# Norm-side weight splits, modulation buffers and transposes of a two-block fp32 network in another order

## The chip, the cores and the metric

The kernel runs on one core of a Trainium2 chip. The metric is the device time of one execution in microseconds; the kernel before was run three times. TensorE multiplies, VectorE, ScalarE and GpSimd do the elementwise work, and SyncE (SP) issues nearly all DMAs from one queue that is served in order. Each engine works through its own row of instructions in a fixed order and waits on semaphores for the others.

## The reference

The input is 512 tokens of width 1024, a context of 256 tokens, and weights, all in fp32. The first block has two layers; the context goes through the first of them and is only read by the second.

```python
for l in range(2):
    mod = silu(c) @ w_mod[l] + b_mod[l]                      # six rows: shift, scale, gate, twice
    px = (rmsnorm(x, norm1_g) * (1 + sc1) + sh1) @ w_in      # mLSTM, gating unit, convolution from px
    x = x + g1 * (y_x @ w_out)
    x = x + g2 * swiglu(rmsnorm(x, norm2_g) * (1 + sc2) + sh2, w_gu, w_down)
x = rmsnorm(x, final_g)
for i in range(2):                                           # mixer A: 3 dilated windows; mixer B: sinks
    h = mixer_a(x, ...) if i == 0 else mixer_b(x, ...)
    x = layer_norm(ALPHA * x + h, ln_g[i], ln_b[i])
    gate = sigmoid(x @ ple_w_gate[i])
    x = x + gate * (p[i] @ ple_w_proj[i])
```

## The kernel before

**Products.** Every fp32 factor is split into a high part (rounded to the format that TensorE takes at full rate) and the rest, the low part; a product is the sum of three matmuls (high by high, high by low, low by high). For a weight block, `wblock` loads it in two halves of 128 x 1024 (`raw`, three buffers), ScalarE copies `hi` (L121) and VectorE subtracts `lo` (L124). Activations are split into `Hh` and `Hl` after they have been transposed on TensorE (`finish_T`, L354; `split_T`, L417; `to_T`, L397). Matmuls and transposes are recorded on the lines of these helpers, L138 for all matmuls.

**Tokens.** They are worked on in chunks of 128: six in layer 0 (four of the input, two of the context), four from then on. `pend` holds functions that transpose and split a chunk once its norm is there; `pend.upto(c)` issues those up to chunk c, so its place in the code says where the transposes stand among TensorE's matmuls.

**Order.** The code is written as one program, and a scheduler places the instructions of each engine by priority, by code order first; `behind(es)` holds the instructions of a block back until the last split recorded for ScalarE ("A") or VectorE ("V") or the last GpSimd instruction ("G") has been issued. Loads are asked for on SP in the order in which the code reaches them, and each waits until its buffer is free.

**The places of the change, in the order of the program.** (1) The FFN of each layer starts with a product that is interleaved with the transposes of its last chunks: `fm_pair` in layer 0, `fm_pairs` in layer 1; `fm_pair` also computes mixer B's keys. (2) `mod_gen` computes one of the six modulation rows: four loads of 1 MB into one buffer `wm`, and 16 small matmuls (32 columns of weights wide) on each; these groups (`md<-wm`) are strewn through the FFN by `modl.pump`. (3) `resid` multiplies a product by the gate row on VectorE (`ot`) and adds it to the residual stream `w` on GpSimd, in quarters of 256 columns. (4) `chunkf` is the norm behind layer 1: scale and gain in two halves, VectorE one, ScalarE and GpSimd the other; the chunk is then transposed for mixer A. (5) Mixer A has four quads of heads by three windows, twelve rounds; `a_pieces` gives the products of a round, `a_stages` the attention of it, and `weave` lays the products of a round between the attention of the round before. `first` is the product of the first round, interleaved with the transposes of the last chunks. (6) After each mixer, `post_attention` adds the output product and normalises, and `embed_gate` computes the gate product in two column halves n, each from two weight halves kh. `affine` multiplies a chunk by the layer norm's gain `lg` (GpSimd) and adds its bias `lb` (VectorE); `use` multiplies the gate `pg` with the projected embedding `pq` and adds it to `w`. The block for (n, kh) = (0, 1), `early`, has buffers of its own and is asked for before `embed_gate`. The stage behind mixer A is called gate 0 here, that behind mixer B gate 1.

## Time and profile before

| | us |
|---|---|
| median of 3 runs (lowest, highest) | 2639.34 (2638.47, 2640.25) |
| the profiled execution | 2640.76 |
| its span (and what lies around it) | 2638.7 (2.06) |
| TensorE busy | 2561.2, 97% of the span |
| VectorE, ScalarE, GpSimd busy | 1329.4, 973.2, 572.6 |

The profile is of one execution. The granted clock is a share of TensorE's full speed (2.4 GHz): 1.00, or 0.50 where it is at its lower level of 1.2 GHz; over the whole span it is 0.99. A row of a timeline gives the start, the duration, the engine, the line, the operation with output and inputs, how many follow one another, and in brackets how long the engine was idle before and what ended that. DVE is VectorE, ACT ScalarE, POOL GpSimd.

### The profile page before, as it was taken

Reading aid. Unit: us, or ns where it says so; the run is one execution under the profiler, and the core shown is the slowest. Engines: PE = TensorE matmul, PEld = TensorE weight load, DVE = VectorE, ACT = ScalarE, POOL = GpSimd, SP = SyncE. Lnnn points to the kernel's source line nnn. Section 1 sums busy time; section 2 is a strip of 40 time slices with the busy share of each in tenths; the row PEclk is TensorE's granted clock in tenths of the full one; section 3 lists DMA queues with packets and bytes.
Section 4 is the critical chain, followed back from the end, with each engine's and each line's share of the span. In section 5 each row is a group of like instructions: output and inputs, shape, how many; then the busy total and the mean of one; then the engine's idle time right before and its main releaser. Section 6 shows DMA issues by size and latency. Waiting matters only on the chain.

```text
span 2638.7 us, 39880 instructions
## 1 busy us (share of the span) xinstructions
PE 2561.2 (97%) x15408; PEld 2163.5 (82%) x15408; DVE 1329.4 (50%) x2858; ACT 973.2 (37%) x2034; POOL 572.6 (22%) x614
## 2 busy tenths in 40 slices
PE   7999999999999999999999999999999999989998
PEld 5888788788888888887978888888888888768777
DVE  4675664142323335766543443534454545665666
ACT  3424444021121225345522222434343445434753
POOL 1175532020302013034220120411111111021102
PEclk9999999999999999999999999999999999999999
DMA  8421553443212123227342332433434443524352
GB/s 304 132 72 41 158 197 120 167 148 123 74 56 72 60 67 112 79 77 215 120 156 84 104 100 80 140 105 99 140 111 136 119 135 112 176 92 138 118 168 64
DMA packets 132286, 314.74 MB, mean 119 GB/s; under 512 B 18785, under 2 KB 49089, under 8 KB 132097
## 3 DMA queue, kind: packets, MB, share of 16 engines
q1 hardware_dynamic: 132096, 312.20, 37.7%
q8 instruction: 121, 1.98, 0.3%
q14 instruction: 69, 0.56, 0.1%
HBM read 272.02 MB, written 13.89 MB: 108 GB/s over the span
## 4 chain that ended last, share of the span: by engine, by line
PE 86%; DVE 4%; DMA 4%; ACT 3%; POOL 2%; issue 1%; SPq 0%; DVEq 0%; POOLq 0%; ACTq 0%
PE mm L138 72%; PE md L138 5%; PE tr L138 5%; PE tr L1272 1%; DMA wm<-in_w_mod_dram 1%; DMA t<-mwd 1%; ACT t L121 1%; DVE lo L124 1%; PE tr L354 1%; POOL w L124 1%; DVE w L124 0%; DVE t L124 0%; POOL t L124 0%; ACT hi L121 0%; DMA w<-in_x_dram 0%
## 5 line engine op out<-in xcount | busy, mean ns | idle before, releaser
L138 PE MATMUL mm<-Hh,hi 128*128 128x512 f32 (+1 forms) x2208 | 798.8, 362 | 7.8 <-ACT hi L121 3.9
L138 PE MATMUL mm<-Hl,hi 128*128 128x512 f32 (+1 forms) x2208 | 772.6, 360 | 0.2 <-DVE Hl L124 0.2
L138 PE MATMUL mm<-Hh,lo 128*128 128x512 f32 (+1 forms) x2208 | 712.9, 360 | 1.4 <-DVE lo L124 1.4
L121 ACT ACTIVATE hi<-raw 128x1024 fp32r<-128x1024 f32 (+1 forms) x350 | 341.6, 1003 | 777.4 <-PE mm L138 364.7
L124 DVE TENSOR_TENSOR lo<-raw,hi 128x1024 fp32r<-128x1024 f32 (+1 forms) x350 | 427.9, 1237 | 272.6 <-ACT hi L121 272.5
L138 PEld LDWEIGHTS mm<-Hh,hi 128*128 128x128 f32 x2208 | 416.6, 189 | 99.0 <-ACT hi L121 4.7
L138 PEld LDWEIGHTS mm<-Hl,hi 128*128 128x128 f32 x2208 | 417.3, 189 | 65.3 <-issue 1.6
L138 PEld LDWEIGHTS mm<-Hh,lo 128*128 128x128 f32 x2208 | 381.5, 189 | 49.8 <-issue 4.2
L124 POOL TENSOR_TENSOR w<-w,ot 128x256 f32<-128x256 f32 x200 | 170.7, 877 | 839.9 <-DVE ot L124 838.5
L124 DVE TENSOR_TENSOR sg<-mm,sg 128x512 f32<-128x512 f32 (+1 forms) x132 | 75.9, 600 | 407.4 <-PE mm L138 231.5
L138 PE MATMUL mm<-hi,Hh 128*128 128x256 f32 (+2 forms) x740 | 224.1, 303 | 4.8 <-ACT Hh L121 4.6
L138 PE MATMUL mm<-hi,Hl 128*128 128x256 f32 (+2 forms) x740 | 220.2, 298 | 1.0 <-POOL Hl L124 1.0
L138 PE MATMUL mm<-lo,Hh 128*128 128x256 f32 (+2 forms) x740 | 219.2, 296 | 2.0 <-DVE lo L124 2.0
L124 POOL TENSOR_TENSOR qr<-rt,rt 128x512 f32<-128x512 f32 x58 | 81.7, 1424 | 487.0 <-DVE rt L124 341.6
L138 PEld LDWEIGHTS mm<-hi,Hh 128*128 128x128 f32 x740 | 140.6, 190 | 12.6 <-ACT Hh L121 5.1
L138 PEld LDWEIGHTS mm<-hi,Hl 128*128 128x128 f32 x740 | 140.5, 190 | 6.5 <-issue 1.2
L138 PEld LDWEIGHTS mm<-lo,Hh 128*128 128x128 f32 x740 | 140.4, 190 | 6.3 <-DVE lo L124 2.4
L138 PE MATMUL mm<-hi,ah 128*128 128x512 f32 x352 | 139.7, 397 | 0.0
L138 PE MATMUL mm<-lo,ah 128*128 128x512 f32 x352 | 139.4, 396 | 0.0
L138 PE MATMUL mm<-hi,al 128*128 128x512 f32 x352 | 139.3, 396 | 0.0
L138 PE MATMUL mm<-hi,Yh 128*128 128x256 f32 (+1 forms) x416 | 129.3, 312 | 4.0 <-DVE t L124 2.6
L138 PE MATMUL mm<-hi,Yl 128*128 128x256 f32 (+1 forms) x416 | 128.2, 308 | 0.0
(369 smaller groups left out, 3666.7 us busy)
## 6 DMA issues: line engine op xcount, KB each, us to landing
raw<-in_w_gu_dram SPq DMA_DIRECT2D x88, 512.0 KB
raw<-in_a_in_dram SPq DMA_DIRECT2D x72, 512.0 KB
wm<-in_w_mod_dram SPq DMA_DIRECT2D x24, 1024.0 KB
raw<-in_w_in_dram SPq DMA_DIRECT2D x40, 512.0 KB
raw<-in_w_mod_dram SPq DMA_DIRECT2D x36, 512.0 KB
raw<-in_w_d_dram SPq DMA_DIRECT2D x24, 512.0 KB
raw<-in_w_d_dram SPq DMA_DIRECT2D x40, 256.0 KB
t<-mwd SPq DMA_DIRECT2D x38, 256.0 KB
```

What stands on the lines that cost most here:

```text
L121: return S.activation(o, i, f, **kw)
L124: return (e or V).tensor_tensor(out=o, in0=x, in1=y, op=op)
L138: lasts["P"] = PE.matmul(o, lhsT=l, rhs=r, start=start, stop=stop, **kw).ins
L354: PE.transpose(pt[:, 128 * m:128 * m + 128], src(4 * i + m), ident)
L1272: PE.transpose(pt[:, 128 * i:128 * i + 128], e, ident)
```

## The change

- `fm_pair` issues the transposes of the next two chunks ahead of the second product (m = 1) on the present two, where they stood behind it; `fm_pairs` issues the last chunk's ahead of the second weight block.
- `mod_gen` gets two `wm` buffers.
- `resid` adds the last chunk's quarters 2 and 3 on VectorE, in the residual addition and in the last FFN group; `chunkf` multiplies the last chunk's second half by the gain on VectorE.
- In `first`, the first weight block of mixer A is no longer held behind the last split; the second one is.
- `weave` calls `ahead` before the last piece of a round: it asks for the first weight block of the next round.
- `affine` does both steps on VectorE, held behind its last split; the block (0, 1) of `embed_gate` is made where it is used, behind the last norm's split on ScalarE and VectorE.

```diff
             for q in range(0, n, 256):
-                pend.upto((o + q) // 128 + 1)
                 for m in range(2):
+                    pend.upto((o + q) // 128 + (3 if m else 1))
                     fm_into([pss[m][i][:, q:q + 256]], wb, 128 * m, H, [(o + q, 256)])
...
             for i, wb in enumerate(wbs):
-                pend.upto(first + i if q == 0 else 9)
+                pend.upto(first if i + q == 0 else 9)
                 for m in range(2):
...
             for kh, c in order:
-                if kh not in wb:
-                    wb[kh] = {(0, 0): first, (0, 1): early}.get((n, kh)) or wblock(src[n, kh], nk, 512)
+                if kh not in wb and (n, kh) == (0, 1) and early:
+                    pend.upto(9)
+                    with behind():
+                        wb[kh] = early()
+                elif kh not in wb:
+                    wb[kh] = (n + kh == 0 and first) or wblock(src[n, kh], nk, 512)
                 hi, lo = wb[kh]
...
         for kp in range(8 // kn):
-            wm = (T(pool, [128, 2, 1024], "wm", bufs=1) if pool
+            wm = (T(pool, [128, 2, 1024], "wm", bufs=2) if pool
                   else T(wp, [128, 1024], "raw", bufs=3).rearrange("p (k n) -> p k n", k=1))
...

-        def resid(pool, c, n, ps, g):
+        def resid(pool, c, n, ps, g, final=True):
             tmp = T(pool, [128, 256], "ot", bufs=3)
...
             tt(tmp, ps, g[:, sl], MUL)
-            tt(xt[c][:, sl], xt[c][:, sl], tmp, ADD, e=G)
+            tt(xt[c][:, sl], xt[c][:, sl], tmp, ADD, e=V if final and n >= 2 and c == chs[-1] else G)

...
                 for n in (2 * n2, 2 * n2 + 1):
-                    resid(FP, c, n, ps[:, 256 * (n % 2):256 * (n % 2) + 256], g2[c // 4])
+                    resid(FP, c, n, ps[:, 256 * (n % 2):256 * (n % 2) + 256], g2[c // 4], lastg)
                     if lastg:
...
         act(xt[:, 512:1024], xt[:, 512:1024], AF.Copy, scale=rs)
-        tt(xt[:, 512:1024], xt[:, 512:1024], fg[0][:, 512:1024], MUL, e=G)
+        tt(xt[:, 512:1024], xt[:, 512:1024], fg[0][:, 512:1024], MUL, e=V if c == 3 else G)
         ld(xf[c], xt)
...
         def affine(c):
-            with behind("G"):
-                tt(xt[c], xt[c], lg, MUL, e=G)
-            tt(xt[c], xt[c], lb, ADD)
+            with behind("V"):
+                tt(xt[c], xt[c], lg, MUL)
+                tt(xt[c], xt[c], lb, ADD)

...

-    def weave(pieces, stages):
+    def weave(pieces, stages, ahead=noop):

...
         for i, p in enumerate(pieces):
+            if i == np_ - 1:
+                ahead()
             p()
...
                 if m == 0:
-                    wb[i] = wblock(a["a_in"][g, Q, i], 8, 256)
+                    if i not in wb:
+                        wb[i] = wblock(a["a_in"][g, Q, i], 8, 256)
                     d["p", i, 0] = fm(wb[i], 0, HA, SEGS_X)[0]
...

+            wb[0] = wblock(a["a_in"][g, Q, 0], 8, 256)
             with behind("AV"):
-                wb[0] = wblock(a["a_in"][g, Q, 0], 8, 256)
-            wb[1] = wblock(a["a_in"][g, Q, 1], 8, 256)
+                wb[1] = wblock(a["a_in"][g, Q, 1], 8, 256)
             ps = [mmt() for _ in range(3)]
...
             return [first, qk(1, 1)] + vs
+
+        def ahead():
+            i = 1 if g == 0 else 0
+            wb[i] = wblock(a["a_in"][g, Q, i], 8, 256)
+
+        d["ahead"] = ahead
         return [qk(i, m) for i in ((1, 0) if g == 0 else (0, 1)) for m in range(2)] + vs
...
     quad = None
-    for (Q, g) in its:
+    zt = {}
+
+    def z_ahead():
+        zt["w"] = wblock(a["a_z"][0], 8, 256)
+
+    ds = [{} for _ in its]
+    rounds = [a_pieces(Q, g, d) for (Q, g), d in zip(its, ds)]
+    for k, (Q, g) in enumerate(its):
         if g == 0:
             nquad = {"st": T(S2, [128, 3, 2, 4, 4], "qst", bufs=2)}
-        d = {}
-        pieces = a_pieces(Q, g, d)
+        d, pieces = ds[k], rounds[k]
         if prev is None:
-            for p in pieces:
-                p()
+            weave(pieces, [], ds[k + 1]["ahead"])
         else:
-            weave(pieces, prev + late)
+            weave(pieces, prev + late, ds[k + 1]["ahead"] if k < 11 else z_ahead)
             late = []
...
         prev_qg, prev_quad = (Q, g), nquad
-    zt = {}

...
         def f():
-            if pr % 2 == 0:
+            if pr % 2 == 0 and pr:
                 zt["w"] = wblock(a["a_z"][pr // 2], 8, 256)
...
     early = T(HBp, [128, 2, 4, 512], "Hh", F32R, bufs=1)
-    early = wblock(a["ple_g"][0, 0, 1], 4, 512, (early[:, 0], early[:, 1]))
+    eh = early[:, 0], early[:, 1]
     HB = []
...

-    embed_gate(0, H, PO, xt, affine, done_a, early)
+    embed_gate(0, H, PO, xt, affine, done_a, lambda: wblock(a["ple_g"][0, 0, 1], 4, 512, eh))
     close(PO)
...
     WX = opened("wx", "right")
-    early = wblock(a["ple_g"][1, 0, 1], 4, 512, [T(WX, [128, 4, 512], t, F32R) for t in ("hi", "lo")])
-    embed_gate(1, H, PO, xt, affine, done_b, early)
+    ew = [T(WX, [128, 4, 512], t, F32R) for t in ("hi", "lo")]
+    embed_gate(1, H, PO, xt, affine, done_b, lambda: wblock(a["ple_g"][1, 0, 1], 4, 512, ew))
     close(PO)
```

What this does to the order of the instructions is shown at three places, in the names of the built programs. First SP's queue in layer 0's FFN, at the modulation loads that precede the rows at 520 to 526 us; `wm` are modulation loads, `raw` with `w_d` and `w_gu` FFN weights. Before:

```order
L281 DMA wm_5267<-in_w_mod_dram 128x2x1024
L159 DMA raw_5482<-in_w_d_dram 128x512
L159 DMA raw_5560<-in_w_gu_dram 128x1024
L281 DMA wm_5670<-in_w_mod_dram 128x2x1024
L281 DMA wm_5680<-in_w_mod_dram 128x2x1024
L281 DMA wm_5820<-in_w_mod_dram 128x2x1024
L159 DMA raw_5564<-in_w_gu_dram 128x1024
L159 DMA raw_5707<-in_w_gu_dram 128x1024
L159 DMA raw_5711<-in_w_gu_dram 128x1024
```

After:

```order
L285 DMA wm_5267<-in_w_mod_dram 128x2x1024
...
L285 DMA wm_5670<-in_w_mod_dram 128x2x1024
L159 DMA raw_5482<-in_w_d_dram 128x512
L159 DMA raw_5560<-in_w_gu_dram 128x1024
L285 DMA wm_5680<-in_w_mod_dram 128x2x1024
L285 DMA wm_5820<-in_w_mod_dram 128x2x1024
L285 DMA wm_5830<-in_w_mod_dram 128x2x1024
L159 DMA raw_5564<-in_w_gu_dram 128x1024
L159 DMA raw_5707<-in_w_gu_dram 128x1024
L159 DMA raw_5711<-in_w_gu_dram 128x1024
```

The second load of the group (wm_5680) is still the one behind wm_5670, but each load is now queued one load further ahead of its use, and wm_5830 stands ahead of the FFN weights raw_5564 to raw_5711.

Next ScalarE at the FFN start of layer 1; `xs_12083` is the second half of the last chunk's scaled rows, `hi_12384` the high part of a weight block, `Hh` that of activations. Before:

```order
L121 ACTIVATE t_1767_12057<-tr_12052,modc_15_99,modc_16_100 128x128 x4
L121 ACTIVATE jk_12050,ss_11671<-w_11533 128x256
L121 ACTIVATE Hh_11519<-t_1767_12057 128x4x128
L121 ACTIVATE Hh_11519<-t_1769_12069 128x4x128
L121 ACTIVATE hi_12384<-raw_12386 128x1024
L121 ACTIVATE xs_12083<-w_11533,rs_12078 128x512
L121 ACTIVATE hi_12384<-raw_12390 128x1024
L121 ACTIVATE t_1787_12208<-tr_12203,modc_15_99,modc_16_100 128x128 x4
L121 ACTIVATE Hh_11519<-t_1787_12208 128x4x128
```

After:

```order
L121 ACTIVATE hi_12086<-raw_12092 128x1024
L121 ACTIVATE t_1767_12057<-tr_12052,modc_15_99,modc_16_100 128x128 x4
L121 ACTIVATE Hh_11519<-t_1767_12057 128x4x128
L121 ACTIVATE jk_12050,ss_11671<-w_11533 128x256
L121 ACTIVATE hi_12384<-raw_12386 128x1024
L121 ACTIVATE Hh_11519<-t_1769_12069 128x4x128
L121 ACTIVATE hi_12384<-raw_12390 128x1024
L121 ACTIVATE xs_12083<-w_11533,rs_12078 128x512
L121 ACTIVATE t_1787_12160<-tr_12155,modc_15_99,modc_16_100 128x128 x4
```

`xs_12083`, which the transposes of the last chunk read, has moved behind both halves of `hi_12384`.

Last VectorE in gate 0; `w_20625` to `w_20631` are chunks 0 to 3, `lo_21227` and `lo_21237` the low parts for the second column half. Before:

```order
L124 TENSOR_TENSOR Hl_20617<-t_3158_20992,Hh_20616 128x4x128
L1317 BN_AGGR mv_21011<-lst_20769 128x2
L124 TENSOR_TENSOR lo_21227<-raw_21232,hi_21226 128x1024
L131 TENSOR_SCALAR rv_21014<-mv_21011 128x1
L124 TENSOR_TENSOR lo_21237<-raw_21238,hi_21236 128x1024
L127 SCALAR_TENSOR_TENSOR nb_21017<-mv_21011,rs_21013 128x1
L133 TENSOR_SCALAR w_20631<-w_20631,mv_21011,rs_21013 128x512
L124 TENSOR_TENSOR lo_21237<-raw_21242,hi_21236 128x1024
L133 TENSOR_SCALAR t_3178_21089<-tr_21084,lncol 128x128 x4
L124 TENSOR_TENSOR Hl_20617<-t_3176_21077,Hh_20616 128x4x128
L124 TENSOR_TENSOR w_20625<-w_20625,lb_20622 128x1024
L124 TENSOR_TENSOR w_20627<-w_20627,lb_20622 128x1024
```

After, at the norm and, behind the dots, after the gating of the first column half:

```order
L1321 BN_AGGR mv_21011<-lst_20769 128x2
L131 TENSOR_SCALAR rv_21014<-mv_21011 128x1
L127 SCALAR_TENSOR_TENSOR nb_21017<-mv_21011,rs_21013 128x1
L133 TENSOR_SCALAR w_20631<-w_20631,mv_21011,rs_21013 128x512
L124 TENSOR_TENSOR lo_21227<-raw_21232,hi_21226 128x1024
L133 TENSOR_SCALAR t_3176_21081<-tr_21076,lncol 128x128 x4
L124 TENSOR_TENSOR Hl_20617<-t_3174_21069,Hh_20616 128x4x128
L124 TENSOR_TENSOR w_20625<-w_20625,lg_20621 128x1024
...
L124 TENSOR_TENSOR w_20631<-w_20631,pg_21214 128x256
L124 TENSOR_TENSOR w_20631<-w_20631,pg_21220 128x256
L124 TENSOR_TENSOR lo_21237<-raw_21238,hi_21236 128x1024
L124 TENSOR_TENSOR lo_21237<-raw_21242,hi_21236 128x1024
```

Between the statistics (`mv`) and the scaled chunk 3 no weight's low part is left; `lo_21237` has moved behind the affine steps and the gating of all four chunks.

## Rows read from the trace of the kernel before

**Rows 1.** The page: engine busy line and chain that ended last.

```profile
PE 2561.2 (97%) x15408; PEld 2163.5 (82%) x15408; DVE 1329.4 (50%) x2858; ACT 973.2 (37%) x2034; POOL 572.6 (22%) x614
...
PE 86%; DVE 4%; DMA 4%; ACT 3%; POOL 2%; issue 1%; SPq 0%; DVEq 0%; POOLq 0%; ACTq 0%
```

**Rows 2.** Who waited for whom, TensorE: us in total, times, longest.

```profile
PE md L138 <- DMA wm<-in_w_mod_dram: 6.1, 3, 5.3
...
PE tr L397 <- DVE w L124: 5.3, 1, 5.3
```

**Rows 3.** Stretches: length, busy us of PE, PEld, DVE, ACT, POOL, granted clock, DMA share.

```profile
429.40:432.80 3.40, 3.18 (x15) 3.11 (x15) 2.62 (x3) 2.87 (x4) 1.28 (x1) 0.50 0.64 251
526.50:535.20 8.70, 8.11 (x31) 5.42 (x32) 2.74 (x6) 1.75 (x3) 0.09 (x1) 0.50 0.48 136
1678.70:1685.40 6.70, 4.95 (x22) 4.56 (x23) 6.00 (x7) 4.93 (x7) 2.77 (x2) 0.50 0.29 98
2358.50:2361.30 2.80, 2.80 (x9) 2.33 (x10) 1.47 (x3) 0.60 (x1) 0.00 (x0) 0.50 0.76 281
2593.40:2596.90 3.50, 3.46 (x12) 3.10 (x13) 2.53 (x6) 2.57 (x7) 0.00 (x0) 0.51 0.00 0
```

**Rows 4.** Timeline of TensorE at layer 0's FFN start: start, us, idle before in brackets.

```profile
425.76 0.28 PE L138 MATMUL mm<-Hh,hi 128*128 128x256 f32 x1
...
426.11 1.03 PE L354 MATMUL tr<-ident,xs 128*128 128x128 f32 x8
...
428.96 0.51 PE L138 MATMUL mm<-Hh,hi 128*128 128x256 f32 x2 [1.82 <-ACT Hh L121]
```

**Rows 5.** Timeline at the modulation loads: TensorE, then SyncE's queue.

```profile
520.22 1.07 PE L138 MATMUL md<-wm,cact 128*32 128x256 f32 x16
...
526.54 1.93 PE L138 MATMUL md<-wm,cact 128*32 128x256 f32 x16 [5.25 <-DMA wm<-in_w_mod_dram]
...
521.35 0.38 SPq L281 DMA_DIRECT2D wm<-in_w_mod_dram  x1
```

**Rows 6.** Timeline at layer 1's FFN start: TensorE, then ScalarE.

```profile
1305.35 1.04 PE L354 MATMUL tr<-ident,xs 128*128 128x128 f32 x8
...
1308.21 0.74 PE L138 MATMUL mm<-Hh,hi 128*128 128x256 f32 x4 [1.82 <-ACT Hh L121]
...
1300.56 0.73 ACT L121 ACTIVATE xs<-w,rs 128x512 f32<-128x512 f32 x1 [0.96 <-POOL rs L124]
...
1301.84 1.06 ACT L121 ACTIVATE hi<-raw 128x1024 fp32r<-128x1024 f32 x1 [0.55 <-DMA raw<-in_w_gu_dram]
```

**Rows 7.** Timeline at mixer A's start: TensorE, ScalarE, VectorE.

```profile
1676.79 0.52 PE L417 MATMUL tr<-ident,w 128*128 128x128 f32 x3 [0.70 <-POOL w L124]
...
1679.61 0.58 PE L138 MATMUL mm<-Hh,hi 128*128 128x256 f32 x1 [2.30 <-ACT hi L121]
...
1682.74 0.90 PE L417 MATMUL tr<-ident,w 128*128 128x128 f32 x3 [0.83 <-POOL w L124]
...
1678.52 1.04 ACT L121 ACTIVATE hi<-raw 128x1024 fp32r<-128x1024 f32 x1
...
1675.97 1.28 DVE L124 TENSOR_TENSOR Hl<-tr,Hh 128x512 fp32r<-128x512 f32 x2
```

**Rows 8.** Timeline at the gates: TensorE (three), GpSimd, VectorE (two).

```profile
2328.95 1.09 PE L354 MATMUL tr<-ident,w 128*128 128x128 f32 x8 [2.72 <-DVE w L133]
...
2358.50 0.69 PE L397 MATMUL tr<-ident,w 128*128 128x128 f32 x2 [5.32 <-DVE w L124]
...
2593.45 0.90 PE L354 MATMUL tr<-ident,w 128*128 128x128 f32 x3 [2.73 <-DVE w L133]
...
2333.73 11.44 POOL L124 TENSOR_TENSOR w<-w,lg 128x1024 f32<-128x1024 f32 x4
...
2336.16 11.22 DVE L124 TENSOR_TENSOR w<-w,lb 128x1024 f32<-128x1024 f32 x4 [3.56 <-POOL w L124]
...
2351.12 1.21 DVE L124 TENSOR_TENSOR lo<-raw,hi 128x1024 fp32r<-128x1024 f32 x1
```

## The prediction

> **What bounds the kernel now.** I read the page first. TensorE is busy for 97% of the span and holds 86% of the chain that ended last [rows 1]; so the time is TensorE's work at the clock it was granted, plus the moments in which it had none. The list of who waited for whom names these moments: its entry for modulation weights is 6.1 us in three waits, one of them 5.3, and its entry for the last transposes of the first gate stage is a single wait of 5.3 [rows 2]. Next I cut the span into stretches and looked at the granted clock: behind five of the waits that the change touches it is 0.50 for some 3 to 9 us [rows 3], the 1.2 GHz level instead of 2.4, so that half of such a stretch is lost work. Last I read the timeline around each of these places. The change is seven edits at six places; one after the other:
>
> **1. FFN start of layer 0.** In its first product TensorE ends the matmuls on chunks 2 and 3, does the eight transposes of the last pair's second chunk (426.11, 1.03 us), and then has nothing until ScalarE has split them: 1.82 us [rows 4]. The change puts these transposes 24 matmuls sooner. Three such matmuls take 0.35 us (425.76 to 426.11), so 24 take 2.8, more than the 1.82: the wait goes. The clock is 0.50 from 429.4 to 432.8 [rows 3], 1.7 us of lost work; I count it as regained, since nothing else idles there. Bounds 1.8 to 3.5; taken **+3.5** (plus is time saved).
>
> **2. Two modulation buffers.** The first group of 16 small matmuls ends at 520.22 + 1.07 = 521.29; the next load is asked for at 521.35, since there is one buffer, and TensorE waits 5.25 us for it until 526.54 [rows 5]: a load takes 5.2 us. With two, the order below shows the load of the second group ahead of the group before it, and the 6.1 us of such waits [rows 2] go. Of 526.5 to 535.2 at 0.50 [rows 3], 0.55 us is another wait; (8.7 - 0.55) / 2 = 4.1 comes back with the clock. Against it: the groups now stand closer. A third group stands 4.1 us of matmuls behind the second (counted in the order, at the spacing of step 1), so that it is wanted 4.1 + 1.07 = 5.2 us after its buffer came free, about when its load lands; five places at up to 0.2 us, 1.0 lost. SyncE's queue is in order, so a load that waits for its buffer also holds the FFN weights behind it; these are wanted a whole FFN step later, and I cost that at nothing (rival C if that cover is gone). Bounds +4 to +10.2; taken 6.1 + 4.1 - 1.0 = **+9.2**.
>
> **3. Last chunk's additions on VectorE.** Where layer 0 hands over, two additions of 256 columns now stand on VectorE ahead of the second half of the weights that TensorE waits for. A quarter as wide as a weight's low part of 1.21 us [rows 8], one costs some 0.3 to 0.5. Bounds -2 (with a clock drop) to +0.3; taken **-0.4**.
>
> **4. FFN start of layer 1.** Here the same kind of move makes a new wait. TensorE reaches the transposes of chunk 3 at 1305.35 and waits 1.82 after them [rows 6]. In the changed order they stand 48 matmuls (5.6 us) sooner, at 1299.75. But half of their input is a ScalarE copy that ran at 1300.56; in the changed order ScalarE has a weight copy ahead of it, which waited for its transfer until 1301.84 and ends at 1302.90 [rows 6]. The input is then there at 1302.9 + 0.73 = 1303.6, and TensorE ends its transposes half a microsecond later, at 1304.1 instead of 1299.75 + 1.04: 3.3 us of waiting for 1.82. Bounds -3 (a longer clock drop) to +3.5 (the transfer lands early); taken **-1.5**.
>
> **5. Mixer A's start.** TensorE waits 0.70, 2.30 and 0.83 us, and runs at 0.50 from 1678.7 to 1685.4 with 4.95 busy [rows 3, 7]. The 2.30 is for the first weight block, whose copy ran at 1678.52, right behind the last chunk's squares and with no transfer to wait for [rows 7]. Now this block's splits stand in front of the last norm, on both engines, and 48 matmuls stand between the three transpose blocks. What is left to wait for are the splits of chunk 1, which ended at 1677.25 [rows 7], about 1.9 us after TensorE is free, and 0.3 for the last chunk. So 3.8 - 2.2 = 1.6, plus 4.95 / 2 = 2.5 of clock, plus 0.3 for the first of the waits, which the same splits cover: **+4.4**. Bounds 0 (both engines' new order delays the last norm by as much as it saves) to 6.3.
>
> **6. First weights of the next round asked for ahead.** In the order of the twelve rounds no row moves on any engine except in the first one, counted in step 5: **0**.
>
> **7. Gates.** At gate 0 TensorE waits 2.72 us for the last norm [rows 8]. In the order two low parts of weights (1.21 each) stand on VectorE between its statistics and its scaling; afterwards none. But five matmuls (1.2 us) that covered the wait move behind it: 2.72 - 2.4 + 1.2 = 1.5 remain, **+1.2**. The second wait, 5.32 us at 2358.50, is for the gated rows of chunk 0: they came late since GpSimd multiplied by the norm's gain (11.44 us for four) and VectorE added its bias beside it (11.22 for four, 2.80 each). The same shape with two inputs, a weight's low part, takes 1.21 with GpSimd idle [rows 8]. All eight on VectorE at 1.21 are 9.7 us, and the gated rows of the first half are done some 10 us sooner: the 5.32 goes, and 1.4 of clock (2.8 us at 0.50, [rows 3]). New on VectorE: the low parts of the second block now stand behind all of this gating. From the norm's scaling on VectorE has 22.5 us up to the first of them (1.2 a low part, 2.1 scaling and split of the last transposes, 1.2 a gain, 2.4 two low parts, 4.8 four affine instructions, 6.0 sixteen gating ones of a quarter of the width, 3.6 three affine ones, 1.2 the low part); TensorE has 22.1 (85 matmuls of 512 columns at 0.233, twice the spacing of step 1, and 2.3 of transposes, waits and two more matmuls). I take 0.7 for this wait and 0.3 for the transposes behind it: 5.3 + 1.4 - 1.0 = **+5.7**. At gate 1 the first wait (2.73) is the same, **+1.2**, less **0.3** for the low parts; its clock drop [rows 3] I count as staying, since 1.5 us of waiting does. Gates together +7.8, bounds -2 to +12.
>
> Which of the two rates holds is the choice on which this step rests; I take 1.21, the row nearest in shape. The Trainium skill, "GPSIMD Engine Reference", section Specifications, says that GpSimd's ports to SBUF are shared with VectorE and contend with VectorE instructions that have two SBUF inputs. By that rule the 2.80 is contention and goes with GpSimd's share, as in my sum; were it no contention, the gates would go as in rival A.
>
> **Sum.** 3.5 + 9.2 - 0.4 - 1.5 + 4.4 + 0 + 7.8 = 23.0. The profiled execution took 2640.76 (span 2638.7 and 2.06 around it): 2617.8. It lies 1.42 above the median of 2639.34, so the forecast is 2616.4, **2616**.
>
> **Rivals.**
> A, slower: VectorE becomes late in the gates. If the eight run at the 2.80 of the biases [rows 8], they take 22.4 instead of 9.7, and the low parts of the second block come 12.7 us later at each gate, with TensorE idle before them and a clock drop behind (1.7 each): 23.0 - 25.4 - 3.4 = -5.8, **2645**. It decides from 2.6 us each on. Against it: 1.21 without GpSimd.
> B: the waits go, but the low clock comes anyway, at these or other places: without 1.7 + 4.1 + 2.5 + 1.4 it is 13.3, **2626**. For it: short waits remain at four of the places.
> C: SyncE's queue, held by modulation loads, brings FFN weights late, and step 2 gives back what it gains: 13.8, **2626**. Against it: the distance of a whole FFN step.
> D: all of it, and the drops of steps 4 and gate 1 go as well (1.7 each), and step 4 gives nothing back: 28, **2611**.
> E: new waits of 1 to 3 us at most of the places, as in step 4, eat the gain: within 0.2% of before, about **2637**.
>
> **How the numbers follow.** Forecast 0.49, A 0.04, B 0.17, C 0.08, D 0.16, E 0.06. 0.2% is 5.3 us, about what a measurement of this kernel can tell from no change. The forecast, B, C and D are faster: 0.90; same 0.06; slower 0.04. The range reaches beyond D on one side and over B and C with some of their spread on the other: 2606 to 2631.
>
> **What would show it.** Right: no wait of TensorE for a modulation load above 0.3 us; the 5.32 gone and all eight multiplications and additions near 1.2 us; the wait at layer 1's FFN start now on the transposes and for ScalarE's copy; in mixer A's start no wait for a weight's high part; rounds unchanged. Wrong: affine instructions near 2 us or more (A); stretches at 0.50 of the same number and length as before (B); TensorE waiting for high parts in the FFN steps (C).

## The result, and the profile after

The changed kernel takes 2612.67 us (median of 4 runs, 2611.05 to 2615.0) against 2639.8 (2638.47 to 2642.61) for the kernel before on the same chip: a ratio of 0.9897, 95% interval 0.9885 to 0.9909. On another chip, later, it was 0.9904 (0.9891 to 0.9917). The forecast was 2616, faster by more than 0.2%. By spans 25.8 us went, 2638.7 to 2612.9; the sum had 23.0.

The page of the changed kernel, busy line and chain, answering to [rows 1]:

```profile
PE 2549.6 (98%) x15408; PEld 2156.1 (83%) x15408; DVE 1331.7 (51%) x2875; ACT 970.5 (37%) x2034; POOL 542.7 (21%) x597
...
PE 85%; DVE 5%; DMA 4%; ACT 3%; POOL 2%; issue 1%; SPq 0%; DVEq 0%; POOLq 0%; ACTq 0%
```

TensorE has the same 15408 instructions and is busy for 11.6 us less: that is the clock. Outside them the span had 77.5 us before (2638.7 - 2561.2) and has 63.3 now: 14.2 us of waits. So nearly half of the gain is clock that came back behind waits.

Who waited for whom on TensorE, answering to [rows 2]:

```profile
PE tr L358 <- DVE xs L131: 2.5, 2, 1.4
...
PE tr L358 <- ACT xs L121: 1.8, 1, 1.8
...
PE md L138 <- DMA wm<-in_w_mod_dram: 0.7, 2, 0.5
```

The modulation loads cost 0.7 us in two waits in place of 6.1 in three, and the 5.3 for the gated rows is no longer in the list. The first entry was 0.9 in one wait and the second is new: 1.4 and 1.8 us of them are layer 1's FFN start. Stretches of the changed kernel, columns as in [rows 3]; the first four are layer 0's FFN start, the modulation loads, the end of gate 0 and gate 1's start, the last two layer 1's FFN start and mixer A's start:

```profile
415.40:418.80 3.40, 3.40 (x32) 3.40 (x30) 2.57 (x9) 3.37 (x9) 0.90 (x2) 1.00 0.00 0
516.00:524.00 8.00, 7.45 (x56) 5.08 (x55) 3.56 (x8) 2.22 (x3) 1.19 (x2) 1.00 0.67 246
...
2342.60:2345.40 2.80, 2.08 (x11) 1.82 (x12) 2.12 (x5) 0.60 (x1) 0.00 (x0) 1.00 0.94 266
2567.00:2570.50 3.50, 2.92 (x16) 2.35 (x15) 2.32 (x6) 2.91 (x7) 1.80 (x1) 1.00 0.44 128
...
1290.40:1293.80 3.40, 3.40 (x19) 3.40 (x19) 1.96 (x5) 3.12 (x5) 1.22 (x1) 0.54 0.69 217
1665.70:1669.10 3.40, 3.40 (x18) 3.40 (x18) 3.40 (x5) 2.48 (x5) 0.00 (x0) 0.52 0.38 111
```

Four of the five places of [rows 3] now run at 1.00; mixer A's start still falls, for half as long, and layer 1's FFN start does as it did before. Where the time went, from the starts of the same matmuls in the two traces (us saved; a stage that nothing touched shows the spread):

| stretch | forecast | measured |
|---|---|---|
| up to layer 0's FFN | 0 | -0.2 |
| layer 0's FFN (steps 1, 2) | 12.7 | 14.2 |
| hand-over to layer 1 (step 3) | -0.4 | -0.8 |
| layer 1's mixer (untouched) | 0 | 1.2 |
| layer 1's FFN (step 4) | -1.5 | -1.3 |
| mixer A's start (step 5) | 4.4 | 3.0 |
| rounds (step 6), and up to gate 0 | 0 | 1.4 |
| gate 0 (step 7) | 6.9 | 6.5 |
| gate 1 (step 7) | 0.9 | 1.9 |

The stretches that the change works on add up to 23.5 of the 25.8, against 23.0 in the sum. The 1.4 up to gate 0 can't be put down to the change: in every other profile of this document, the second one of the changed kernel included, the stretch from the end of mixer A's start up to gate 0 is longer than in this one, by 0.1 to 2.7 us.

### The profile page after: what moved, and what is told of

It is laid out like the page before. It is cut to its first block, busy times and chain, and to the rows that moved or that the text cites. A ratio compares the mean times of both kernels' runs of the same rounds, so it can differ in the third digit from the quotient of the medians.

```text
span 2612.9 us, 39877 instructions
## 1 busy us (share of the span) xinstructions
PE 2549.6 (98%) x15408; PEld 2156.1 (83%) x15408; DVE 1331.7 (51%) x2875; ACT 970.5 (37%) x2034; POOL 542.7 (21%) x597
## 4 chain that ended last, share of the span: by engine, by line
PE 85%; DVE 5%; DMA 4%; ACT 3%; POOL 2%; issue 1%; SPq 0%; DVEq 0%; POOLq 0%; ACTq 0%
PE mm L138 72%; PE tr L138 5%; PE md L138 5%; PE tr L1276 2%; DMA wm<-in_w_mod_dram 1%; DVE lo L124 1%; DMA t<-mwd 1%; DVE w L124 1%; ACT t L121 1%; DVE t L124 1%; ACT hi L121 1%; PE tr L358 1%; DMA w<-in_x_dram 0%; DMA raw<-in_w_vg_dram 0%; DMA raw<-in_b_k_dram 0%
## 5 line engine op out<-in xcount | busy, mean ns | idle before, releaser
L124 POOL TENSOR_TENSOR w<-w,ot 128x256 f32<-128x256 f32 x192 | 162.4, 870 | 824.2 <-DVE ot L124 822.9
L124 DVE TENSOR_TENSOR rt<-mm,cs 128x512 f32<-128x512 f32 x116 | 74.9, 684 | 108.2 <-PE mm L138 98.5
```

Source lines behind the costliest of these rows:

```text
L124: return (e or V).tensor_tensor(out=o, in0=x, in1=y, op=op)
```

## The experiments

Each kernel is the changed one with the edit shown; the times of its traces are compared at the starts of the same matmuls. "Idle" is the sum of all gaps ahead of TensorE's matmuls in its profile, "low clock" the sum, over the span in slices of 1 us, of one minus the granted clock.

| kernel | median us (lowest to highest) | ratio to before, 95% | span | idle | low clock |
|---|---|---|---|---|---|
| before | 2639.8 | 1 | 2638.7 | 72.9 | 25.6 |
| changed | 2612.67 (2611.05 to 2615.0) | 0.9897 (0.9885 to 0.9909) | 2612.9 | 58.7 | 12.4 |
| a_changed_again | 2616.39 (2611.81 to 2616.94) | 0.9904 (0.9891 to 0.9917) | 2614.2 | 58.2 | 14.8 |
| u1_old_layer0_start | 2617.85 (2616.04 to 2622.14) | 0.9916 (0.9903 to 0.9930) | 2620.4 | 60.7 | 19.6 |
| u2_one_buffer | 2624.26 (2621.92 to 2625.39) | 0.9933 (0.9920 to 0.9947) | 2622.5 | 62.1 | 18.1 |
| u7_gain_on_gpsimd | 2625.64 (2622.05 to 2628.04) | 0.9940 (0.9928 to 0.9952) | 2626.2 | 67.3 | 17.4 |
| u7_weights_ahead_of_norm | 2618.55 (2613.88 to 2622.13) | 0.9919 (0.9906 to 0.9933) | 2612.1 | 58.5 | 12.8 |
| u7_both_undone | 2623.06 (2619.88 to 2629.69) | 0.9935 (0.9922 to 0.9948) | 2624.2 | 66.2 | 18.7 |
| u4_old_layer1_start | 2613.08 (2612.08 to 2614.43) | 0.9894 (0.9880 to 0.9907) | 2612.3 | 57.7 | 13.7 |
| u5_old_mixer_start | 2614.41 (2612.35 to 2616.34) | 0.9898 (0.9885 to 0.9912) | 2610.5 | 57.1 | 10.2 |
| c45_old_starts | 2612.78 (2610.56 to 2614.78) | 0.9894 (0.9881 to 0.9908) | 2612.5 | 57.3 | 12.8 |
| u3_adds_on_gpsimd | 2608.65 (2607.02 to 2609.85) | 0.9879 (0.9865 to 0.9892) | 2607.8 | 54.3 | 11.9 |
| u3_adds_only | 2610.3 (2605.78 to 2613.05) | 0.9883 (0.9870 to 0.9896) | 2604.0 | 54.1 | 9.2 |
| c3_pairs | 2612.34 (2609.57 to 2616.68) | 0.9889 (0.9875 to 0.9903) | 2614.9 | 57.1 | 14.6 |

Span less the two last columns is 2539 to 2543 in every row: waits and clock are all that moves. One kernel's runs spread over 2 to 10 us, and most stretches of low clock cost 1.7 us (3.4 us at 0.50), so differences of 2 us are read from the place in the trace, not from the median. The runs were made on several chips; a ratio is to the kernel before on the same chip, where its median was 2639.8 to 2641.07.

### Layer 0's FFN: transposes and buffers

```diff
-                for m in range(2):
-                    pend.upto((o + q) // 128 + (3 if m else 1))
+                pend.upto((o + q) // 128 + 1)
+                for m in range(2):
```

> The changed kernel with the transposes at layer 0's FFN start at their old places; all else as changed. By step 1 the time goes up by 3.5 us: the wait of 1.8 us at the transposes is back, and the stretch at half clock behind it (1.7 us of lost work). Rival B: the low clock comes without the wait too, at one of the next waits; then only 1.8 us are lost.

TensorE at that place in this kernel, timeline:

```profile
425.80 1.03 PE L358 MATMUL tr<-ident,xs 128*128 128x128 f32 x8
...
428.66 0.50 PE L138 MATMUL mm<-Hh,hi 128*128 128x256 f32 x2 [1.82 <-ACT Hh L121]
```

The 1.82 is back as in [rows 4], and so is the low clock (1.70 us in the slices from 430 to 434). Against the changed kernel's trace it loses 3.7 us between 388 and 495. Step 1 said 3.5. The median is 5.2 above the changed kernel's first and 1.5 above its second.

```diff
-            wm = (T(pool, [128, 2, 1024], "wm", bufs=2) if pool
+            wm = (T(pool, [128, 2, 1024], "wm", bufs=1) if pool
```

> The changed kernel with one modulation buffer again instead of two; all else as changed. By the prediction's step 2 the time goes up by about 9 us (the waits for modulation weights, about 6, and 4 of lost clock behind the long one, less the 0.7 us of new small waits), from 2612.7 to about 2622. If the low clock came anyway, whatever the waits (rival B), it goes up by about 5.5, to 2618. If two buffers cost something elsewhere by holding SyncE's queue (rival C), taking one away gives that back: less than 5 us up, and the FFN weights of layer 0 land earlier than with two.

The wait in TensorE's timeline, then the stretch around and behind it (columns as in [rows 3]):

```profile
522.22 1.93 PE L138 MATMUL md<-wm,cact 128*32 128x256 f32 x16 [5.36 <-DMA wm<-in_w_mod_dram]
```

```profile
521.00:530.00 9.00, 7.23 (x29) 4.74 (x30) 2.15 (x4) 1.15 (x2) 0.00 (x0) 0.50 0.37 130
```

The wait of [rows 5] is back, with 5.1 us of low clock: 1.0 of it falls into this wait and the 0.55 behind it, when TensorE had nothing to do, so 4.1 of work are lost to it. The median is 11.6 above the first median of the changed kernel, 7.9 above the second; in the trace 11.1 are lost inside layer 0's FFN. So by the trace it is more than the theory's 9, and rival B's 5.5 falls. The waits for modulation loads (6.2 against 0.7) and the 4.1 make 9.7 of it; where the other 1.4 went is not shown. Rival C falls too: with two buffers TensorE waits for no high part of a weight anywhere in that FFN. All its waits there, from 420 to 1000 us:

```profile
PE md L138 <- DMA wm<-in_w_mod_dram: 0.7, 2, 0.5
PE md L138 <- DVE mb L124: 0.5, 1, 0.5
```

### The gates: two edits that need each other

First the multiplication by the norm's gain goes back to GpSimd:

```diff
-            with behind("V"):
-                tt(xt[c], xt[c], lg, MUL)
-                tt(xt[c], xt[c], lb, ADD)
+            with behind("G"):
+                tt(xt[c], xt[c], lg, MUL, e=G)
+            tt(xt[c], xt[c], lb, ADD)
```

> The changed kernel with the norm's gain multiplied on GpSimd again in both gates, the second half of the weights still split behind the last norm. If contention with GpSimd sets the biases' 2.80 us (step 7 and the rule beside it), they are back at 2.5 us or more, the rows of the first half come late, the wait of about 5 us at gate 0's last transposes is back with its clock, and the time goes up by 5 to 7 us, to about 2619. If the order of the weights' splits made the gain, the biases may slow down but the time goes up by less than 2 us.

The four biases of gate 0 on VectorE: count, shortest/median/longest in ns, first and last start. First the changed kernel, with its gains on VectorE too, then this one, with the gains on GpSimd:

```profile
L124 DVE TENSOR_TENSOR w<-w,lg x4: 1212/1216/1218, 2312.7 to 2326.1; 128x1024 f32<-128x1024 f32 x4
...
L124 DVE TENSOR_TENSOR w<-w,lb x4: 1212/1215/1218, 2317.2 to 2328.6; 128x1024 f32<-128x1024 f32 x4
```

```profile
L124 DVE TENSOR_TENSOR w<-w,lb x4: 1209/3420/3433, 2320.5 to 2330.5; 128x1024 f32<-128x1024 f32 x4
...
L124 POOL TENSOR_TENSOR w<-w,lg x4: 3374/3390/3404, 2316.1 to 2326.1; 128x1024 f32<-128x1024 f32 x4
```

Beside GpSimd's multiplication a bias takes 3.42 us; the one that ran after the last of them, and all in the changed kernel, take 1.21. GpSimd's own, 2.40 at the shortest before, take 3.39. The kernel before had the same two rates, in the same view of its gate 0:

```profile
L124 DVE TENSOR_TENSOR w<-w,lb x4: 1211/3410/3421, 2336.2 to 2346.2; 128x1024 f32<-128x1024 f32 x4
```

The 2.80 of the prediction is the mean of a merged row: three of its four took 3.40 to 3.42 and the last, with GpSimd done, 1.21. Shortest, median and longest would have told both rates apart before any run. In u7_gain_on_gpsimd the delay reaches TensorE at gate 0 and at gate 1 (timeline):

```profile
2320.60 0.50 PE L138 MATMUL mm<-Hh,Hh 128*128 128x512 f32 x1 [1.16 <-DVE Hh L124]
...
2335.59 0.50 PE L138 MATMUL mm<-lo,Hh 128*128 128x512 f32 x1 [2.13 <-DVE lo L124]
...
2343.14 0.69 PE L401 MATMUL tr<-ident,w 128*128 128x128 f32 x2 [3.11 <-DVE w L124]
...
2587.03 0.50 PE L138 MATMUL mm<-lo,Hh 128*128 128x512 f32 x1 [1.15 <-DVE lo L124]
...
2601.99 0.50 PE L138 MATMUL mm<-lo,Hh 128*128 128x512 f32 x1 [2.07 <-DVE lo L124]
```

The kind of loss is the one expected, the size is not: 9 to 13 us by the two medians of the changed kernel, 8.3 at gate 0 and 3.1 at gate 1 in the trace, where 5 to 7 were expected. The low parts now stand behind the norm, in the middle of the contention, so they are stretched and late too (the two of gate 0's first column half take 4.82 us here, 3.46 in the changed kernel). This is rival A's mechanism, which the change avoids by keeping GpSimd out.

Next only the split of the second half of the weights goes back ahead of the last norm (the block is again made by the caller and handed over), the gain staying on VectorE:

```diff
-                if kh not in wb and (n, kh) == (0, 1) and early:
-                    pend.upto(9)
-                    with behind():
-                        wb[kh] = early()
-                elif kh not in wb:
-                    wb[kh] = (n + kh == 0 and first) or wblock(src[n, kh], nk, 512)
+                if kh not in wb:
+                    wb[kh] = {(0, 0): first, (0, 1): early}.get((n, kh)) or wblock(src[n, kh], nk, 512)
```

> The changed kernel with the second half of the gate's weights split ahead of the last norm again in both gates, the norm's gain and bias still on VectorE. By step 7 the wait for the last norm grows back from 1.4 to 2.7 us at each gate (1.2 more each), and the two small waits behind it at gate 0 (0.97 and 0.78 us) shrink or go (1.0 to 1.7 less): the time goes up by 1 to 2 us, about 3.5 if a half-clock stretch comes back at gate 1. Rival: the split's place is worth as much as VectorE's taking over the gain; then it goes up by 5 us or more.

Timeline of this kernel at the two gates, and under it the changed kernel's:

```profile
2308.06 1.09 PE L354 MATMUL tr<-ident,w 128*128 128x128 f32 x8 [2.72 <-DVE w L133]
...
2358.52 0.39 PE L138 MATMUL mm<-Hl,hi 128*128 128x256 f32 x1 [0.98 <-DVE Hl L124]
...
2566.52 1.97 PE L354 MATMUL tr<-ident,w 128*128 128x128 f32 x8 [2.73 <-DVE w L133]
```

```profile
2308.51 0.66 PE L358 MATMUL tr<-ident,w 128*128 128x128 f32 x4 [0.82 <-DVE w L133]
2309.67 0.66 PE L358 MATMUL tr<-ident,w 128*128 128x128 f32 x4 [0.51 <-ACT w L121]
2332.36 0.50 PE L138 MATMUL mm<-lo,Hh 128*128 128x512 f32 x1 [0.97 <-DVE lo L124]
2343.32 0.44 PE L401 MATMUL tr<-ident,w 128*128 128x128 f32 x2 [0.78 <-DVE w L124]
...
2566.51 0.66 PE L358 MATMUL tr<-ident,w 128*128 128x128 f32 x4 [0.81 <-DVE w L133]
2567.75 0.66 PE L358 MATMUL tr<-ident,w 128*128 128x128 f32 x4 [0.58 <-ACT w L121]
```

The first waits grow to 2.72 and 2.73 as expected; at gate 0 the two small waits go. In the trace this costs 0.5 us at gate 0 and 1.6 at gate 1, where the low clock of [rows 3] is back (1.7 in the slices from 2565). The median is 2 to 6 us above the changed kernel's, so the rival's 5 is not excluded by the median alone; by the trace the theory's 1 to 2 holds. Last, both edits undone, the two diffs together:

> The changed kernel with both gate edits undone: the norm's gain on GpSimd and the second half of the weights split ahead of the last norm. By step 7 the two together gave 7.8 us, by the two traces 9.8: about 2620.5 to 2622.5. The gain's edit alone cost 13 when undone and the split's alone 2 to 6; if the two are separate gains they sum to 15 or more, 2628; if the split behind the norm is a loss as long as GpSimd multiplies, undoing both costs less than undoing the first alone.

By the trace it loses 7.8 at gate 0 and 1.9 at gate 1, 9.7 in all; TensorE's waits at gate 0 are the old ones:

```profile
2313.09 1.55 PE L354 MATMUL tr<-ident,w 128*128 128x128 f32 x8 [2.72 <-DVE w L133]
...
2342.58 0.69 PE L397 MATMUL tr<-ident,w 128*128 128x128 f32 x2 [4.00 <-DVE w L124]
```

Against 11.4 for undoing the gain alone: as long as GpSimd multiplies, splitting behind the norm loses 1.7 us (11.4 - 9.7); once it doesn't, it saves 2.1. The gain's move alone is worth 7.6 (9.7 - 2.1). The 1.7 is the size of one stretch of low clock and rests on one profile of each; the medians, 2625.64 and 2623.06, point the same way, their intervals overlap. TensorE's waits at the two gates, which leave the clock out, say it more clearly: 4.5 us in the changed kernel (3.1 to 4.7 in all profiles with its gates), 6.4 with the split ahead of the norm, 13.4 with the gain on GpSimd and 10.3 with both. So behind the norm the split saves some 2 us of waiting without GpSimd's multiplication and costs 3.1 beside it.

### Layer 1's FFN start and mixer A's start

First the transposes, then the splits, back to their old places:

```diff
-                pend.upto(first if i + q == 0 else 9)
+                pend.upto(first + i if q == 0 else 9)
```

> The changed kernel with the transposes at layer 1's FFN start at their old places; all else as changed. By step 4 this was a loss: the wait of 3.2 us goes back to about 1.8, so the time goes down by 1.4 to 3 us (the upper end if the half-clock stretch behind the wait goes too), to about 2610 to 2611. Rival: the low clock comes at either place and ScalarE's wait for its transfer is met anyway; then the time is the same within 0.5 us.

```diff
-            wb[0] = wblock(a["a_in"][g, Q, 0], 8, 256)
             with behind("AV"):
-                wb[1] = wblock(a["a_in"][g, Q, 1], 8, 256)
+                wb[0] = wblock(a["a_in"][g, Q, 0], 8, 256)
+            wb[1] = wblock(a["a_in"][g, Q, 1], 8, 256)
```

> The changed kernel with the splits of mixer A's first weight block behind the last norm again and those of the second block free, as before; all else as changed. By step 5 the time goes up by 4.4 us; by the trace of the changed kernel, where the clock fell at this place after all, by about 3, to 2615.7, and the wait for the first weight's high part (2.3 us) is back. Rival: the gain at this place came from the transposes of the last chunk and not from the order of the splits; then it goes up by less than 1 us.

Both together:

> The changed kernel with both the transposes at layer 1's FFN start and the first two weight splits of mixer A's start at their old places. Each alone took 1.4 and 0.9 us off the changed kernel's way up to the next stage in its trace, by the positions of TensorE's instructions. If these add up the time goes down by 2.3 us, to about 2610.5, and the profile shows at mixer A's start one wait of 2.5 us for the first weight's high part and no half clock behind it. Rival: the half-clock stretches come and go from run to run; then the time is the changed kernel's within 1 us.

None of the three medians differs by more than 2 us from the changed kernel's first one. At its place the first saves 1.4 us, as step 4 would have it. The second does not lose 4.4 or 3: it saves 0.9. So the rival of u5_old_mixer_start, a gain of less than 1 us from the order of the splits, is nearest, and step 5's mechanism falls, at least as the order of the splits alone. Mixer A's start with the old order (one row), then in the changed kernel, timelines:

```profile
1662.83 0.39 PE L138 MATMUL mm<-Hh,hi 128*128 128x256 f32 x1 [2.54 <-ACT hi L121]
```

```profile
1663.30 0.66 PE L138 MATMUL mm<-Hh,hi 128*128 128x256 f32 x2 [1.09 <-ACT Hh L121]
1665.05 0.39 PE L138 MATMUL mm<-Hl,hi 128*128 128x256 f32 x1 [1.09 <-DVE Hl L124]
```

With the old order the wait for the first high part is back, 2.54 for the 2.30 of [rows 7], but the 0.70 and 0.83 for GpSimd's rows are not, and no low clock follows. What else differs there from the kernel before is the last chunk's work, which VectorE now does. And the changed kernel's second wait, 1.09, is for a split on VectorE; its rows around it:

```profile
1662.71 0.75 DVE L124 TENSOR_TENSOR ot<-mm,g 128x256 f32<-128x256 f32 x2
1663.37 1.02 DVE L124 TENSOR_TENSOR w<-w,ot 128x256 f32<-128x256 f32 x1
1664.31 1.27 DVE L124 TENSOR_TENSOR Hl<-tr,Hh 128x512 fp32r<-128x512 f32 x2
1665.51 0.41 DVE L124 TENSOR_TENSOR w<-w,ot 128x256 f32<-128x256 f32 x1
```

One of the moved additions stands ahead of that split and takes 1.02 us, while the next one takes 0.41. That led to the next three runs. In c45_old_starts the two savings did not add up: mixer A's start has the one wait of 2.54 and no low clock, as expected, but there is 0.99 of a new wait behind it, and the median is the same.

### The last chunk's additions

```diff
-            tt(xt[c][:, sl], xt[c][:, sl], tmp, ADD, e=V if final and n >= 2 and c == chs[-1] else G)
+            tt(xt[c][:, sl], xt[c][:, sl], tmp, ADD, e=G)
...
-        tt(xt[:, 512:1024], xt[:, 512:1024], fg[0][:, 512:1024], MUL, e=V if c == 3 else G)
+        tt(xt[:, 512:1024], xt[:, 512:1024], fg[0][:, 512:1024], MUL, e=G)
```

> The changed kernel with the last chunk's additions, and the final norm's last multiplication, on GpSimd again; all else as changed. By step 3 of the prediction this edit cost 0.4 us where layer 0 hands over, so the time goes down by about 0.4. Rival, formed after the run with mixer A's old start: the edit is what took away two of the three waits there (0.70 and 0.83 us, both for GpSimd's rows, and the clock behind them); then these waits are back and the time goes up by 1.5 to 3.2 us.

The first hunk alone:

> The changed kernel with only the last chunk's additions on GpSimd again; the final norm's last multiplication stays on VectorE. If the additions are what costs (1.02 us each on VectorE beside GpSimd's multiplication where others take 0.41, ahead of the split that TensorE waits for), nearly all of the 4 us that both edits gave back is here: about 2609, and mixer A's start has one wait of 1.09 us in place of two. If it is the multiplication, the time stays at the changed kernel's.

Both hunks, and the transposes of layer 1's FFN start at their old places:

> Additions and multiplication on GpSimd, and the transposes at layer 1's FFN start at their old places; all else as changed. If step 4 still costs something with the additions gone, about 2607.5; if the early transposes have become harmless, since VectorE no longer delays the last norm there, 2609 or up to 1 us more.

Both theories on u3 were wrong in size, and the rival in sign: it is faster, 2608.65, all its runs below all eight of the changed kernel's (the intervals of the ratios, 0.9865 to 0.9892 and 0.9885 to 0.9909, just overlap). At three of the four places where the additions run, the hand-over, layer 1's FFN start and mixer A's start, its trace saves 7.2 us against the changed kernel's. Mixer A's start there, TensorE and VectorE:

```profile
1657.39 0.67 PE L138 MATMUL mm<-Hh,hi 128*128 128x256 f32 x2 [1.09 <-ACT Hh L121]
...
1656.80 0.75 DVE L124 TENSOR_TENSOR ot<-mm,g 128x256 f32<-128x256 f32 x2
1657.46 1.28 DVE L124 TENSOR_TENSOR Hl<-tr,Hh 128x512 fp32r<-128x512 f32 x2
```

The split follows at once, the second wait is gone, no low clock follows, and the two waits for GpSimd's rows stay away: with the new order of the splits 48 matmuls stand between the transposes, which is why, it seems, they are covered. So for those two waits the splits' order and the additions each suffice, which is why undoing either showed nothing; the two alone undone together were not run (the kernel before, with every edit undone, has both waits). Layer 1's FFN start, ScalarE, in the changed kernel and then in u3:

```profile
1283.41 1.06 ACT L121 ACTIVATE hi<-raw 128x1024 fp32r<-128x1024 f32 x1 [0.55 <-DMA raw<-in_w_gu_dram]
...
1287.91 1.06 ACT L121 ACTIVATE hi<-raw 128x1024 fp32r<-128x1024 f32 x1 [2.92 <-DMA raw<-in_w_gu_dram]
1288.87 0.71 ACT L121 ACTIVATE xs<-w,rs 128x512 f32<-128x512 f32 x1
```

```profile
1282.15 1.05 ACT L121 ACTIVATE hi<-raw 128x1024 fp32r<-128x1024 f32 x1
1284.16 0.72 ACT L121 ACTIVATE xs<-w,rs 128x512 f32<-128x512 f32 x1 [0.96 <-POOL rs L124]
1285.18 1.06 ACT L121 ACTIVATE hi<-raw 128x1024 fp32r<-128x1024 f32 x1 [0.30 <-DMA raw<-in_w_gu_dram]
```

With the additions on GpSimd the copy that the transposes need again stands ahead of the one that waits for its transfer. In u4, with the old places but the additions on VectorE, it stands behind it. So what set the trap of step 4 is the additions' move, by way of the order that follows from it; the early transposes are what meets it, since u4, with that order and late transposes, waits 1.88 in place of 3.2. u3 has one wait of 1.20 here, u3_adds_only one of 1.38, c3_pairs the old 1.82: without the trap the early transposes gain about half a microsecond. c3_pairs, at 2612.34, is slower than both its theories (2607.5, and 2609 to 2610). Its trace is 6.3 us longer than u3's between the first matmuls and the last, but only 1.1 of that lies at layer 1's FFN start; most of the rest is spread over stretches ahead of it that its edit leaves alone. u3_adds_only shows that the additions are nearly all of it; its runs overlap with the changed kernel's on the same chip (median 2610.3 against 2616.39). At those three places its trace saves 4.6 us. It has neither of the two second waits, but 0.47 and 0.99 of others a few us behind mixer A's start; c45_old_starts has the 0.99 too. Both keep the multiplication on VectorE, but so do the changed kernel and u5_old_mixer_start, which have neither wait, so their cause stays open. The multiplication's own part, the difference of 2608.65 and 2610.3, is not clear of noise.

### The changed kernel again

> The changed kernel itself, to stand on the same chip as the three below. About 2612.7 us, within 2. If the half-clock stretches and the second wait at layer 1's FFN start (for ScalarE's copy behind the copy that waits for its transfer) are a matter of when the transfer lands, they may be there or not; if they belong to the order alone, both waits (1.4 and 1.8 us) and the stretch behind them are there again.

The median, 2616.39, is 3.7 us above the first one, more than the 2 expected; the two profiles differ by 0.5 us between the first matmuls and the last, so where the rest of the 3.7 went is not shown. Layer 1's FFN start has 1.44 and 0.94 (1.41 and 1.79 the first time), with the low clock behind. In the eight profiles that have this order the second wait is 2.07, 1.79, 1.76, 1.54, 0.94, 0.72, 0.40 and 0.38, as the transfer lands later or earlier; behind the two shortest no low clock follows, behind the other six it does. So the second wait comes from the order, and its length from the landing.

## Why the prediction was right, and where it was not

The time was right, 2616 for 2612.67, and the two large steps held in kind and size. That it was this close is partly luck: step 2 brought more than its term and steps 3 and 5 less, and 2.4 us of the gain lie in stretches that the change does not touch.

- **Step 1** (3.5): 3.7 when undone.
- **Step 2** (9.2): 11.1 when undone. Small new waits cost 0.7, not 1.0; the clock behind the wait was worth 4.1, as in the sum. The 1.4 that neither explains stays open.
- **Step 3** (-0.4): the sum looked at layer 0's hand-over only, where it fits: the second wait there is 1.73 in the changed kernel, 1.38 or 1.39 in the three with the additions on GpSimd, and was 1.39 before. The same line also runs at layer 1's FFN start and mixer A's start, and the prediction did not cost it there. That is the step that failed: undone, it saves about 4 us by the first median, 4.6 and 7.2 at the places in the two traces.
- **Step 4** (-1.5): -1.3, and the copy behind the waiting copy is in the trace as described. But that ScalarE's copy stands there is the additions' doing, not the transposes'. The first of the two waits, 1.41, was missed. It ends with VectorE's scaling of the same rows, which takes 1.49 us beside GpSimd, but that slowness is not all of it: where the scaling takes 0.48 and 0.49, in u3_adds_on_gpsimd and u3_adds_only, the wait is 1.20 and 1.38.
- **Step 5** (4.4): 3.0, and for a reason only half right. The waits left add up to the 2.2 of the forecast by luck: 1.09 and 1.09, where 1.9 and 0.3 were summed, and one of them is for a split behind an addition, not for the chunk's splits as such; and the clock, taken as regained, fell again, for half as long.
- **Step 6** (0): the rounds' three waits (0.73, 0.54 and 0.48) are the same in both traces. No run undoes this step alone.
- **Step 7** (7.8): 8.4 between the two traces, 9.7 when undone. First waits 1.33 and 1.39 for 1.5; low parts 0.97 for 0.7; transposes 0.78 for 0.3; gate 1's low clock, taken as staying, went. The choice of 1.21 over 2.80 decided it, and u7_gain_on_gpsimd shows the price of leaving GpSimd in; 2.80 itself was a mean over three at 3.41 and one at 1.21. The Trainium skill, "GPSIMD Engine Reference", section Specifications, names this contention for VectorE instructions in a two-port mode or with two SBUF inputs; the traces agree for the biases, which have two such inputs (1.21 and 3.42). A scaling with one tensor input was slowed as well (0.49 and 1.49); whether it ran in such a mode no run shows.

Of the rivals, B had a true part: low clock came at a place where it was counted as gone (mixer A's start), and went at one where it was counted as staying. A is real as a mechanism, but the change removes its cause. C and E show nothing. D's extras came in part: gate 1's low clock.

## What to carry to other kernels

Moving a small SBUF-to-SBUF operation from GpSimd to VectorE is not free where GpSimd still works beside it: cost it at every place where the line runs, with the rate beside GpSimd, and look at what stands behind it. Moving all of a chain off GpSimd pays (7.6 us here), moving single additions cost about 4. A mean over merged instructions can hide two rates: look at the shortest and the longest before it is put into a sum. And two edits at one place are not a sum: undo each alone and both, since one can be a loss until the other is there.

## What the runs showed of the hardware

- VectorE beside GpSimd: additions of 256 columns took 1.02 and 1.07 us in place of 0.41, a scaling of 512 columns 1.49 in place of 0.49. Each ended 0.27 to 0.29 us after GpSimd's instruction did. The scaling at layer 1's FFN start, the same operation on the chunk before, and GpSimd's split beside the first (1285.07 + 1.78 = 1286.85; 1285.64 + 1.49 = 1287.13), timelines of the changed kernel:

```profile
1285.64 1.49 DVE L131 TENSOR_SCALAR xs<-w,rs 128x512 f32<-128x512 f32 x1
...
1276.05 0.49 DVE L131 TENSOR_SCALAR xs<-w,rs 128x512 f32<-128x512 f32 x1 [0.73 <-POOL rs L124]
...
1285.07 1.78 POOL L124 TENSOR_TENSOR Hl<-t,Hh 128x512 fp32r<-128x512 f32 x1 [0.24 <-ACT Hh L121]
```

  It is not always VectorE that loses: at the hand-over an addition of the same shape took 0.42 (at 1004.36 in the changed kernel) while a split of the shape above on GpSimd was under way, and that split took 3.17. Instructions with an input from PSUM kept their time beside GpSimd (0.68 for such a split, 0.42 for a multiplication).
- Low clock follows waits loosely. At mixer A's start two waits of 1.09, 0.7 us of work apart, had it behind them in seven of eight profiles; one wait of 2.54 in neither of two, one of 1.09 in none of three. Gate 1's start had it in all three profiles in which TensorE waited 2.71 to 2.73 there and in none in which it was two waits of together about 1.4. Gate 0's start, with the same wait of 2.72, had it in one of three (u7_both_undone, 1.7 of the 7.8 lost there). Which run has which stretch is a good part of the spread of the times.
